# Latent attention block: rotation of q and filler low parts on VectorE, modulation strips in two buffers of their own

## The chip, the core and the metric

One core of a Trainium2 chip runs the kernel: TensorE (PE) for matmuls and transposes, VectorE (DVE), ScalarE (ACT) and GpSimd (POOL) for element work, SyncE (SP) as the queue that issues DMA. The metric is the device time of one execution in microseconds, the median of several.

## The reference

A decoder block on 512 tokens of width 1024, in fp32. A conditioning vector gives six modulation vectors; a merged w_in feeds a latent attention (MLA) and a sparse attention (NSA); a SwiGLU feed-forward (FFN) follows.

```
mod = silu(c) @ ada_w + ada_b                    # 1024 x 6144: shift, scale, gate, twice
h = rms_norm(x) * (1 + sc1) + sh1
z = h @ w_in                                     # c_q 768, c_kv 256, k_pe 32, NSA inputs, two merge gates
q = (rms_norm(c_q) @ w_q_b).reshape(S, 8, 96)    # 64 plain + 32 rotary columns a head
kv = (rms_norm(c_kv) @ w_kv_b).reshape(S, 8, 128)
q, k = rms_norm(q), rms_norm([kv[:64], k_pe])
q[64:96], k[64:96] = apply_rope(...)             # x1*cos - x2*sin, x2*cos + x1*sin
y_mla = causal_attention(q, k, v) @ w_o_mla
merged = sigmoid(g_mla) * y_mla + sigmoid(g_nsa) * y_nsa
x = x + gt1 * (merged @ w_out)
h2 = rms_norm(x) * (1 + sc2) + sh2
x = x + gt2 * ((silu(h2 @ w_gate) * (h2 @ w_up)) @ w_down)
```

## The kernel before

Every fp32 matmul is made of three in a shorter format: an operand is split into a high part (`whi`, `cTh`, `phi`, ..., by ScalarE) and a low part (`wlo`, `cTl`, `plo`, ..., the difference, by VectorE or GpSimd), and high x high, low x high and high x low are added in PSUM. A weight is loaded in pieces of 512 or 384 KB by `wchunk` into a ring of four `raw` buffers (pool `wp`) and split there.

The program runs in stages: modulation and w_in (0 to 162 us of the span), NSA (162 to 304), the latent projections (304 to 362), the eight MLA heads (362 to 452), the output product of MLA and the merge (452 to 484), w_out and the second norm (484 to 536), the FFN (536 to 904). In the projections `latent_cols` transposes the latents (`cTh`, `cTl`), `gk` is the product with w_kv_b and `gq` that with w_q_b, each for two halves c of four heads and four token tiles t. `use_kv` turns a `gk` tile into `msk` (sums of squares), `kn` and `VM`; `use_q` turns a `gq` tile into `jq` (squares, two buffers), `msq` and `qn`. `norm_q` makes the scale `rsq` out of `msq` by a chain of small operations (`rq_i_q`, `rq_h_q`, `rq_m_q`, 128x16 each). In a head, `qh`/`ql` and `kh`/`kl` are the transposed q and k, `ps` the scores, `s`/`mn` the masked scores and their row minimum (a custom operation and a read of its accumulator), `sm` the sums, `av` the values.

Work of other stages is woven in as filler: the merge gates' products (`gp`), the NSA output product (`yn`), and `mods`, the modulation vectors still to come. `fill_lo` chooses the engine for the low parts of a filler's weight, in pieces of 128x512. `mods` goes through 32 strips of 512 KB of ada_w; a strip needs two `macc` operations on VectorE (128x512, accumulator += strip x one element of silu(c) a partition). `E_MODS`, `F_MODS`, `Y_MODS` and `W_MODS` are how many strips the code offers to the projections, heads, merge (twice that) and w_out; `need_mod` runs what is still missing before a vector is used.

The order on each engine is not that of the code: a scheduler that walks through the program with its own estimate of durations sets it, under the dependences and under the pacing of the fillers. Engines and SyncE's queue then work strictly in that order. In the listings L144 before and L143 after are the helper that records every operation of an engine, so its tile names tell operations apart.

Of the kernel before, what the change touches and what calls it, by code (L numbers as in the profile page):

```python
# [35 lines left out]
EF_POOL = 1  # L36
# [5 lines left out]
E_MODS = 4  # L42
F_MODS = 4
GS_BUFS = 1
Y_MODS = 4
W_MODS = 4
# [68 lines left out]
def hybrid_block(ctx, tc, a, out):  # L115
# [152 lines left out]
    def rows(w, r0, parts, c0, n):  # L268
        return w[r0 : r0 + parts * P, c0 : c0 + n].rearrange("(a p) n -> p a n", p=P)

    fill_at = [0, 1]

    def fill_lo():
        fill_at[0] += 1
        return dve if fill_at[0] % fill_at[1] else pool, FILL_CUT
# [618 lines left out]
    strip_src = {}  # L894

    def strip():
        if "pool" in strip_src:
            return strip_src["pool"].tile([P, 1024], F32, name="strip", tag="strip", bufs=1)
        return wp.tile([P, 1024], F32, name="raw", tag="raw")

    mods_done = set()

    def mods():
# [25 lines left out]
        for m, slot in ((2, 4), (3, 2), (4, 3), (5, 5)):  # L929
            done = finish if slot < 4 else finish_row  # L930
            for hf in range(2):
                acc = mcp.tile([P, S], F32, name="macc", tag="macc", bufs=2)
                for r0 in range(0, KD, 2):
                    raw = strip()
                    sp.dma_start(out=raw.rearrange("p (r n) -> p r n", r=2), in_=rows(ada, r0 * P, 2, m * D + hf * S, S))
                    for r in range(2):
                        src = raw[:, r * S : (r + 1) * S]
                        c = csil[:, r0 + r : r0 + r + 1]
                        if r0 + r == 0:
                            dve.tensor_scalar(out=acc, in0=src, scalar1=c, scalar2=None, op0=ALU.mult)  # L940
                        else:
                            dve.scalar_tensor_tensor(out=acc, in0=src, scalar=c, in1=acc, op0=ALU.mult, op1=ALU.add)
                    if r0 == MOD_LAG and late:
                        finish_last(late)
                    yield
                late.append((done, acc, m, slot, hf))
# [115 lines left out]
    fill_at[1] = EF_POOL  # L1062
# [9 lines left out]
    with tc.tile_pool(name="mp", bufs=1, side="right", reuse_waits="tile") as mp:  # L1072
# [36 lines left out]
        def use_q(c):  # L1109
            hs = slice(4 * c, 4 * c + 4)  # L1110

            def f(t, ps):
# [3 lines left out]
                act.activation(out=qn[t][:, hs, :], in_=pv, func=AF.Copy)  # L1116
                dve.tensor_reduce(out=msq[:, c, t, :], in_=jq, axis=AX.X, op=ALU.add)
                rope(pool, qn[t][:, hs, 64:96], c2q[:, t, :], snq[:, t, 16:32], snq[:, t, 0:16], mp, f"q{t}")
# [470 lines left out]
    strip_src["pool"] = fp  # L1589
# [77 lines left out]
```

## Time and profile before

| | us |
|---|---|
| median of 3 runs (lowest to highest) | 907.83 (907.36 to 909.1) |
| profiled execution | 906.09 |
| its span in the trace | 904.0 |
| TensorE busy | 855.2 (95%) |
| VectorE busy | 636.0 (70%) |
| ScalarE busy | 432.4 (48%) |
| GpSimd busy | 176.3 (20%) |

The span is the time from the first to the last record of the trace; the execution's own time has 2.1 us more around it. Busy times are sums over the span. PEclk in the rows below is the TensorE clock that was granted in a stretch, as a share of full speed. "idle before <-releaser" names what ended an engine's wait.

### The profile page before, as it was taken

The page shows a single profiled execution, that of the slowest core. Times are in us where ns is not written, and L with a number is a line of the kernel's source. Part 1 is how long each engine was busy: PE and PEld are TensorE (multiplying, and loading weights), DVE is VectorE, ACT ScalarE, POOL GpSimd, SP SyncE. Part 2 cuts the span into 40 slices and gives each one's busy share as a digit, 9 for nine tenths or more (in the row PEclk, how much of TensorE's full clock was granted, in tenths as well). Part 3 has the DMA queues.
Part 4 walks back from the last instruction along what each step waited for, and adds up shares of the span by engine and source line. Part 5 has one row for each costly group of instructions (what it writes and reads, how often), then busy time and mean ns, then how long its engine had stood idle before and what let it go on. Part 6 is the DMA issues. An engine that isn't in the chain of part 4 may idle for free.

```text
span 904.0 us, 13055 instructions
## 1 busy us (share of the span) xinstructions
PE 855.2 (95%) x4676; PEld 731.4 (81%) x4676; DVE 636.0 (70%) x1288; ACT 432.4 (48%) x863; POOL 176.3 (20%) x222
## 2 busy tenths in 40 slices
PE   5999899899999997999999989999999999999997
PEld 4879899677777786787777878888899889988986
DVE  5857786778976788578779898866754565555644
ACT  5335654787764644466654345341344224431440
POOL 0003335434432037231148014000000000000000
PEclk9999999999999999699999999999999999999999
DMA  9934445321100654135488671553233313342312
GB/s 317 303 98 130 138 140 140 82 71 46 49 12 24 213 150 140 58 106 152 154 293 287 213 229 43 168 163 94 69 106 121 103 53 112 94 119 91 94 47 94
DMA packets 98116, 115.48 MB, mean 128 GB/s; under 512 B 6548, under 2 KB 70660, under 8 KB 98052
## 3 DMA queue, kind: packets, MB, share of 16 engines
q1 hardware_dynamic: 97956, 114.62, 41.3%
q8 instruction: 37, 0.61, 0.3%
q14 instruction: 27, 0.22, 0.1%
q10 hardware_dynamic: 96, 0.03, 0.0%
HBM read 106.24 MB, written 8.39 MB: 127 GB/s over the span
## 4 chain that ended last, share of the span: by engine, by line
PE 73%; DVE 13%; DMA 7%; ACT 2%; issue 2%; SPq 1%; POOL 1%; DVEq 0%; POOLq 0%; ACTq 0%
PE d L144 14%; PE fu L144 13%; PE gp L144 9%; PE fx L144 6%; PE ga L144 5%; PE fy L144 4%; PE pt L144 4%; PE av L144 3%; DMA raw<-in_ada_w_dram 3%; PE fg L144 3%; PE wa L144 2%; DVE macc L144 2%; PE gwo L144 2%; DVE wlo L144 2%; PE ps L144 2%
## 5 line engine op out<-in xcount | busy, mean ns | idle before, releaser
L144 ACT ACTIVATE whi<-raw 128x1024 fp32r<-128x1024 f32 (+4 forms) x162 | 142.1, 892 | 183.0 <-PE d L144 57.8
L144 DVE TENSOR_TENSOR wlo<-raw,whi 128x1024 fp32r<-128x1024 f32 (+3 forms) x122 | 144.0, 1184 | 73.5 <-ACT whi L144 73.1
L144 PE MATMUL fu<-h2l,whi 128*128 128x512 f32 (+1 forms) x192 | 71.3, 372 | 0.0
L144 PE MATMUL fu<-h2h,whi 128*128 128x512 f32 (+1 forms) x192 | 70.7, 372 | 0.0
L144 PE MATMUL fu<-h2h,wlo 128*128 128x512 f32 (+1 forms) x192 | 69.9, 373 | 0.0
L144 PE MATMUL d<-whi,mh 128*128 128x512 f32 x176 | 69.8, 398 | 0.0
L144 PE MATMUL d<-wlo,mh 128*128 128x512 f32 x176 | 69.6, 395 | 0.0
L144 PE MATMUL d<-whi,ml 128*128 128x512 f32 x176 | 67.0, 394 | 0.0
L144 ACT ACTIVATE s<-s,mn 128x384 f32<-128x384 f32 (+2 forms) x96 | 52.5, 548 | 23.0 <-DVE mn L144 22.3
L144 DVE TENSOR_TENSOR plo<-pt,phi 128x512 fp32r<-128x512 f32 (+2 forms) x78 | 46.1, 601 | 21.5 <-ACT phi L144 21.1
L144 POOL TENSOR_TENSOR wlo<-raw,whi 128x512 fp32r<-128x512 f32 x40 | 52.3, 1329 | 44.4 <-ACT whi L144 44.4
L144 PE MATMUL gp<-hTh,whi 128*128 128x512 f32 x128 | 55.4, 433 | 3.7 <-ACT qn L144 3.7
L144 ACT ACTIVATE phi<-pt 128x512 fp32r<-128x512 f32 (+2 forms) x78 | 40.1, 526 | 31.8 <-PE pt L144 31.4
L144 PE MATMUL gp<-hTh,wlo 128*128 128x512 f32 x128 | 52.0, 406 | 0.0
L144 PE MATMUL gp<-hTl,whi 128*128 128x512 f32 x128 | 51.6, 404 | 0.0
L144 DVE SCALAR_TENSOR_TENSOR macc<-raw,csil,macc 128x512 f32<-128x512 f32 x45 | 37.1, 829 | 8.8 <-DMA raw<-in_ada_w_dram 8.3
L144 PEld LDWEIGHTS fu<-h2l,whi 128*128 128x128 f32 x192 | 36.2, 189 | 6.1
L144 PEld LDWEIGHTS fu<-h2h,whi 128*128 128x128 f32 x192 | 35.9, 189 | 6.0
L144 PEld LDWEIGHTS fu<-h2h,wlo 128*128 128x128 f32 x192 | 35.6, 189 | 5.5
L144 PEld LDWEIGHTS d<-whi,mh 128*128 128x128 f32 x176 | 33.0, 188 | 8.2 <-issue 0.2
L144 PEld LDWEIGHTS d<-whi,ml 128*128 128x128 f32 x176 | 33.0, 188 | 8.1
L144 PEld LDWEIGHTS d<-wlo,mh 128*128 128x128 f32 x176 | 33.0, 188 | 7.9 <-issue 0.2
(427 smaller groups left out, 2427.6 us busy)
## 6 DMA issues: line engine op xcount, KB each, us to landing
raw<-in_ada_w_dram SPq DMA_DIRECT2D x26, 512.0 KB, 4.3
raw<-in_ffn_w_gate_dram SPq DMA_DIRECT2D x22, 512.0 KB, 4.7
raw<-in_ffn_w_up_dram SPq DMA_DIRECT2D x22, 512.0 KB, 3.8
raw<-in_ffn_w_down_dram SPq DMA_DIRECT2D x22, 512.0 KB, 4.9
araw<-in_ada_w_dram SPq DMA_DIRECT2D x32, 256.0 KB, 6.3
raw<-in_w_in_dram SPq DMA_DIRECT2D x16, 512.0 KB, 3.9
spill<-gs SPq DMA_DIRECT2D x24, 256.0 KB, 2.0
raw<-in_w_in_dram SPq DMA_DIRECT2D x12, 352.0 KB, 3.2
```

What stands on the lines that cost most here:

```text
L144: out = call(*args, **kw)
```

## The change

`use_q` leaves GpSimd: VectorE multiplies the rotary columns by sine and cosine straight from the PSUM tile `gq` (`rot`, two products of 128x4x16; `qn`, one of 128x4x32) and adds `rot` in SBUF; ScalarE copies only the other 64 columns of each head. On GpSimd these were four operations a tile (`rp_q` twice, two on `qn`), eight tiles. After NSA the low parts of filler weights go to VectorE (16 pieces of 128x512), where GpSimd did them. The strips of `mods` get a pool tag of their own, `strip`, with two buffers, in place of the shared `raw` ring (and of one buffer in a pool of the FFN), and the load of a strip is issued one step before its two `macc`. The numbers of strips offered to the stages change: 4, 4, 2x4, 4 become 0, 16, 2x3, 2.

```diff
--- before.py
+++ after.py
@@ -33,17 +33,16 @@
 YM_AHEAD = 1
 PACE_Y = 8
 FETCH_AHEAD = 4
-EF_POOL = 1
 MOD_LAG = 2
 D_GATES = 88
 E0_GATES = 8
 E_GATES = 0
 F_FILL = 64
-E_MODS = 4
-F_MODS = 4
+E_MODS = 0
+F_MODS = 16
 GS_BUFS = 1
-Y_MODS = 4
-W_MODS = 4
+Y_MODS = 3
+W_MODS = 2
 BIG = 1e30
 QL = 768
 KVL = 256
@@ -268,11 +267,10 @@
     def rows(w, r0, parts, c0, n):
         return w[r0 : r0 + parts * P, c0 : c0 + n].rearrange("(a p) n -> p a n", p=P)
 
-    fill_at = [0, 1]
+    fill_on = [pool]
 
     def fill_lo():
-        fill_at[0] += 1
-        return dve if fill_at[0] % fill_at[1] else pool, FILL_CUT
+        return fill_on[0], FILL_CUT
 
     turn_at = [0]
 
@@ -891,13 +889,6 @@
                         spill(ps, 16 + 2 * i + j)
                     yield
 
-    strip_src = {}
-
-    def strip():
-        if "pool" in strip_src:
-            return strip_src["pool"].tile([P, 1024], F32, name="strip", tag="strip", bufs=1)
-        return wp.tile([P, 1024], F32, name="raw", tag="raw")
-
     mods_done = set()
 
     def mods():
@@ -926,24 +917,33 @@
             pe.matmul(pm, ones, acc, start=True, stop=True)
             dve.tensor_tensor(out=o, in0=pm, in1=o, op=ALU.add)
 
-        for m, slot in ((2, 4), (3, 2), (4, 3), (5, 5)):
-            done = finish if slot < 4 else finish_row
-            for hf in range(2):
+        slots = ((2, 4), (3, 2), (4, 3), (5, 5))
+        jobs = [(m, slot, hf, r0) for m, slot in slots for hf in range(2) for r0 in range(0, KD, 2)]
+
+        def load(job):
+            m, slot, hf, r0 = job
+            raw = mcp.tile([P, 2, S], F32, name="strip", tag="strip", bufs=2)
+            sp.dma_start(out=raw, in_=rows(ada, r0 * P, 2, m * D + hf * S, S))
+            return raw
+
+        ready = load(jobs[0])
+        for i, (m, slot, hf, r0) in enumerate(jobs):
+            raw = ready
+            if i + 1 < len(jobs):
+                ready = load(jobs[i + 1])
+            if r0 == 0:
                 acc = mcp.tile([P, S], F32, name="macc", tag="macc", bufs=2)
-                for r0 in range(0, KD, 2):
-                    raw = strip()
-                    sp.dma_start(out=raw.rearrange("p (r n) -> p r n", r=2), in_=rows(ada, r0 * P, 2, m * D + hf * S, S))
-                    for r in range(2):
-                        src = raw[:, r * S : (r + 1) * S]
-                        c = csil[:, r0 + r : r0 + r + 1]
-                        if r0 + r == 0:
-                            dve.tensor_scalar(out=acc, in0=src, scalar1=c, scalar2=None, op0=ALU.mult)
-                        else:
-                            dve.scalar_tensor_tensor(out=acc, in0=src, scalar=c, in1=acc, op0=ALU.mult, op1=ALU.add)
-                    if r0 == MOD_LAG and late:
-                        finish_last(late)
-                    yield
-                late.append((done, acc, m, slot, hf))
+            for r in range(2):
+                c = csil[:, r0 + r : r0 + r + 1]
+                if r0 + r == 0:
+                    dve.tensor_scalar(out=acc, in0=raw[:, r], scalar1=c, scalar2=None, op0=ALU.mult)
+                else:
+                    dve.scalar_tensor_tensor(out=acc, in0=raw[:, r], scalar=c, in1=acc, op0=ALU.mult, op1=ALU.add)
+            if r0 == MOD_LAG and late:
+                finish_last(late)
+            yield
+            if r0 == KD - 2:
+                late.append((finish if slot < 4 else finish_row, acc, m, slot, hf))
         yield
         yield
         finish_last(late)
@@ -1059,7 +1059,7 @@
     nsa_last = pe.log[-1]
     spill_src.clear()
     pe.pace = 0
-    fill_at[1] = EF_POOL
+    fill_on[0] = dve
     tab_st.close()
 
     mc_st = scope()
@@ -1113,9 +1113,15 @@
                 pv = ps.rearrange("p (h d) -> p h d", h=4)
                 jq = mp.tile([P, 4, MQK], F32, name="jq", tag="jq", bufs=2)
                 act.activation(out=jq, in_=pv, func=AF.Square)
-                act.activation(out=qn[t][:, hs, :], in_=pv, func=AF.Copy)
+                act.activation(out=qn[t][:, hs, 0:64], in_=pv[:, :, 0:64], func=AF.Copy)
+                rot = mp.tile([P, 4, 32], F32, name="rot", tag="rot", bufs=2)
+                heads = lambda v: v.unsqueeze(1).broadcast_to([P, 4, v.shape[-1]])
+                qr = qn[t][:, hs, 64:96]
+                dve.tensor_tensor(out=rot[:, :, 0:16], in0=pv[:, :, 80:96], in1=heads(snq[:, t, 0:16]), op=ALU.mult)
+                dve.tensor_tensor(out=rot[:, :, 16:32], in0=pv[:, :, 64:80], in1=heads(snq[:, t, 16:32]), op=ALU.mult)
+                dve.tensor_tensor(out=qr, in0=pv[:, :, 64:96], in1=heads(c2q[:, t, :]), op=ALU.mult)
+                dve.tensor_tensor(out=qr, in0=qr, in1=rot, op=ALU.add)
                 dve.tensor_reduce(out=msq[:, c, t, :], in_=jq, axis=AX.X, op=ALU.add)
-                rope(pool, qn[t][:, hs, 64:96], c2q[:, t, :], snq[:, t, 16:32], snq[:, t, 0:16], mp, f"q{t}")
             return f
 
         def norm_q(c):
@@ -1586,7 +1592,6 @@
     mg_st.close()
     h2s = ctx.enter_context(tc.tile_pool(name="h2s", bufs=1, reuse_waits="tile"))
     fp = ctx.enter_context(tc.tile_pool(name="fp", bufs=1, side="right", reuse_waits="tile"))
-    strip_src["pool"] = fp
     for k0 in range(0, KD, 4):
         early.append(wchunk(rows(wg, k0 * P, 4, 2 * P, 256), 4, 256))
     sg_first = gu_finish(0, ps_first)
```

What the scheduler makes of it at three places follows. First VectorE at the start of the projections, from the last latent columns (`cTl`) to the first sums of squares (`msk`), before:

```order
L144 SCALAR_TENSOR_TENSOR cTl_3724<-pt,cols_701,cTh_3723 128x512
L144 SCALAR_TENSOR_TENSOR cTl_3760<-pt,cols_701,cTh_3759 128x512
L144 TENSOR_TENSOR wlo<-raw,whi 128x1024
L144 TENSOR_SCALAR macc<-raw,csil 128x512
L144 SCALAR_TENSOR_TENSOR cTl_3745<-pt,cols_701,cTh_3744 128x512
L144 SCALAR_TENSOR_TENSOR macc<-raw,csil,macc 128x512
L144 TENSOR_TENSOR wlo<-raw,whi 128x1024
L144 SCALAR_TENSOR_TENSOR macc<-raw,csil,macc 128x512
L144 TENSOR_REDUCE msk<-jq 128x4
L144 SCALAR_TENSOR_TENSOR VM_3504<-gk_3569,rkv,VM_3504 128x4x64
```

and now, at the same place:

```order
L143 SCALAR_TENSOR_TENSOR macc<-strip,csil,macc 128x512
L143 SCALAR_TENSOR_TENSOR cTl_3719<-pt,cols_701,cTh_3718 128x512
L143 SCALAR_TENSOR_TENSOR cTl_3755<-pt,cols_701,cTh_3754 128x512
L143 SCALAR_TENSOR_TENSOR macc<-strip,csil,macc 128x512
L143 TENSOR_TENSOR wlo<-raw,whi 128x1024
L143 SCALAR_TENSOR_TENSOR cTl_3740<-pt,cols_701,cTh_3739 128x512
L143 TENSOR_TENSOR wlo<-raw,whi 128x1024
L143 TENSOR_TENSOR wlo<-raw,whi 128x768
L143 SCALAR_TENSOR_TENSOR macc<-strip,csil,macc 128x512
L143 TENSOR_SCALAR macc<-strip,csil 128x512
L143 SCALAR_TENSOR_TENSOR macc<-strip,csil,macc 128x512 x2
L143 TENSOR_REDUCE msk<-jq 128x4
```

With four further up, two of them ahead of the first `cTl`, six `macc` stand now ahead of the first `wlo`, and ten ahead of the first `msk`; before it was none and three.

Second SyncE's queue at the end of NSA, where w_kv_b for the projections is loaded. Before:

```order
L924 DMA gt_4638<-in_ada_b_dram 128x512 x2
L257 DMA raw<-in_mla_w_kv_b_dram 128x2x512
L935 DMA raw<-in_ada_w_dram 128x2x512
L864 DMA spill_1847<-gs 128x512
L257 DMA raw<-in_mla_w_kv_b_dram 128x2x512
L935 DMA raw<-in_ada_w_dram 128x2x512
L257 DMA raw<-in_mla_w_q_b_dram 128x2x384 x3
```

and now:

```order
L926 DMA strip<-in_ada_w_dram 128x2x512 x2
L915 DMA gt_4517<-in_ada_b_dram 128x512 x2
L926 DMA strip<-in_ada_w_dram 128x2x512
L256 DMA raw<-in_mla_w_kv_b_dram 128x2x512 x2
L862 DMA spill_1847<-gs 128x512
L256 DMA raw<-in_mla_w_q_b_dram 128x2x384
L926 DMA strip<-in_ada_w_dram 128x2x512
```

Three strips stand now ahead of w_kv_b; the third needs a buffer that the first one's two `macc` give back.

Third VectorE up to the first score operation (`ISA s`) of the first head. Before, its last rows:

```order
L144 SCALAR_TENSOR_TENSOR ql<-pt,cols_701,qh 96x512
L144 TENSOR_TENSOR rq_m_q_4281<-rq_i_q_4279,rq_h_q_4280 128x16
L144 TENSOR_TENSOR rq_m_q_4281<-rq_m_q_4281,rq_i_q_4279 128x16
L144 SCALAR_TENSOR_TENSOR kl<-pt,cols_701,kh 96x512
L144 SCALAR_TENSOR_TENSOR rsq<-rq_m_q_4281,rq_i_q_4279 128x16
L144 SCALAR_TENSOR_TENSOR macc<-raw,csil,macc 128x512 x2
L144 ISA s_4136,mn<-ps,mask,rsq 128x128
```

and now, the rows from the scale `rsq` of the first four heads on, as far as the second four's `msq`:

```order
L143 SCALAR_TENSOR_TENSOR rsq<-rq_m_q_3926,rq_i_q_3924 128x16
L143 TENSOR_TENSOR wlo<-raw,whi 128x512 x4
L143 TENSOR_REDUCE msq<-jq 128x4
L143 TENSOR_TENSOR rot<-gq_3940,snq 128x4x16 x2
L143 TENSOR_TENSOR qn_3498<-gq_3940,c2q 128x4x32
L143 TENSOR_REDUCE msq<-jq 128x4
L143 TENSOR_TENSOR rot<-gq_3941,snq 128x4x16 x2
L143 TENSOR_TENSOR qn_3499<-gq_3941,c2q 128x4x32
L143 TENSOR_TENSOR wlo<-raw,whi 128x512
L143 TENSOR_TENSOR qn_3498<-qn_3498,rot 128x4x32
L143 TENSOR_TENSOR wlo<-raw,whi 128x512
L143 SCALAR_TENSOR_TENSOR msq<-msq,vq 128x16
```

The two `macc` in front of the score are gone from that place; six `wlo` of filler weights and the rotation of the last two `gq` tiles stand now between `rsq` and the scores. Counted over the whole of VectorE's order, `macc` operations up to the first MLA score operation are 16 (14 before), up to the first `gm` 44 (30), the last `gm` 48 (34), the first `tm` 56 (40), the first `xs` 64 (52); there are 64 in all.

## Rows read from the trace of the kernel before

**Rows 1.** The page's head: the span, busy time of each engine (share of the span, instructions), and the chain that ended last by engine.

```profile
span 904.0 us, 13055 instructions
...
PE 855.2 (95%) x4676; PEld 731.4 (81%) x4676; DVE 636.0 (70%) x1288; ACT 432.4 (48%) x863; POOL 176.3 (20%) x222
...
PE 73%; DVE 13%; DMA 7%; ACT 2%; issue 2%; SPq 1%; POOL 1%; DVEq 0%; POOLq 0%; ACTq 0%
```

**Rows 2.** Busy time of each engine in stretches of the span: start and end, length, then busy time and number of instructions of each engine, the granted clock, the busy share of DMA, GB/s.

```profile
304.00:362.00 58.00, 48.78 (x248) 42.61 (x246) 52.24 (x124) 30.41 (x66) 24.52 (x40) 0.97 0.54 164
362.00:452.00 90.00, 85.19 (x440) 70.14 (x441) 63.10 (x157) 54.37 (x134) 18.94 (x18) 0.92 0.38 118
...
480.00:536.00 56.00, 50.54 (x227) 40.61 (x225) 52.51 (x76) 24.20 (x42) 15.46 (x10) 0.97 0.75 240
...
610.00:904.00 294.00, 289.37 (x1578) 250.09 (x1576) 169.59 (x231) 94.33 (x123) 0.00 (x0) 1.00 0.30 92
```

**Rows 3.** VectorE's timeline, first half of the projections: start, duration, operation, number of them, and in brackets the idle time before and what ended it.

```profile
300.36 2.07 DVE L144 SCALAR_TENSOR_TENSOR cTl<-pt,cols,cTh 128x512 fp32r<-128x512 f32 x3 [1.15 <-ACT cTh L144]
304.13 2.73 DVE L144 SCALAR_TENSOR_TENSOR cTl<-pt,cols,cTh 128x512 fp32r<-128x512 f32 x4 [1.71 <-ACT cTh L144]
...
309.01 0.74 DVE L144 SCALAR_TENSOR_TENSOR macc<-raw,csil,macc 128x512 f32<-128x512 f32 x1
309.70 1.23 DVE L144 TENSOR_TENSOR wlo<-raw,whi 128x1024 fp32r<-128x1024 f32 x1
...
312.01 0.48 DVE L144 SCALAR_TENSOR_TENSOR VM<-gk,rkv,VM 128x256 fp32r<-128x256 f32 x1
...
317.87 0.75 DVE L144 SCALAR_TENSOR_TENSOR macc<-raw,csil,macc 128x512 f32<-128x512 f32 x1 [0.49 <-DMA raw<-in_ada_w_dram]
...
326.88 0.75 DVE L144 SCALAR_TENSOR_TENSOR macc<-raw,csil,macc 128x512 f32<-128x512 f32 x1 [2.23 <-DMA raw<-in_ada_w_dram]
...
328.58 0.90 DVE L144 TENSOR_TENSOR kn<-kpr,rsk 128x128 f32<-128x128 f32 x4
...
329.73 1.43 DVE L144 TENSOR_TENSOR kn<-kn,rsk 128x256 f32<-128x256 f32 x4
331.08 1.15 DVE L144 TENSOR_TENSOR kn<-kpr,rsk 128x128 f32<-128x128 f32 x4
...
335.28 2.06 DVE L144 TENSOR_TENSOR kn<-kn,rsk 128x256 f32<-128x256 f32 x4
```

**Rows 4.** The same, second half, up to the first score operation (CUSTOM_DVE_ANT_0).

```profile
341.56 0.17 DVE L144 SCALAR_TENSOR_TENSOR rq_i_q<-rq_m_q,rq_i_q 128x16 f32<-128x16 f32 x1
341.77 1.31 DVE L144 TENSOR_TENSOR rq_m_q<-rq_i_q,rq_h_q 128x16 f32<-128x16 f32 x1
343.11 1.22 DVE L144 TENSOR_TENSOR rq_m_q<-rq_m_q,rq_i_q 128x16 f32<-128x16 f32 x1
344.36 1.21 DVE L144 SCALAR_TENSOR_TENSOR rq_i_q<-rq_m_q,rq_i_q 128x16 f32<-128x16 f32 x1
345.61 1.20 DVE L144 TENSOR_TENSOR rq_m_q<-rq_i_q,rq_h_q 128x16 f32<-128x16 f32 x1
...
356.35 0.38 DVE L144 TENSOR_TENSOR rq_m_q<-rq_m_q,rq_i_q 128x16 f32<-128x16 f32 x1
...
359.50 2.41 DVE L144 SCALAR_TENSOR_TENSOR macc<-raw,csil,macc 128x512 f32<-128x512 f32 x2
361.83 0.34 DVE L144 CUSTOM_DVE_ANT_0 s<-ps,mask,rsq 128x128 f32<-128x128 f32 x1
```

**Rows 5.** GpSimd's timeline in the same stretch.

```profile
341.75 5.03 POOL L144 TENSOR_TENSOR wlo<-raw,whi 128x512 fp32r<-128x512 f32 x4 [1.36 <-ACT whi L144]
...
359.91 3.14 POOL L144 TENSOR_TENSOR wlo<-raw,whi 128x512 fp32r<-128x512 f32 x2 [1.95 <-ACT whi L144]
```

**Rows 6.** TensorE's timeline: the matmuls behind its two longest waits.

```profile
350.43 0.50 PE L144 MATMUL gp<-hTh,whi 128*128 128x512 f32 x1 [3.69 <-ACT qn L144]
...
362.23 0.69 PE L144 MATMUL ps<-kh,qh 96*128 96x384 f32 x1 [2.85 <-DVE mn L144]
```

**Rows 7.** Busy times by stretch, as in rows 2, in shorter stretches.

```profile
350.00:362.00 12.00, 8.96 (x38) 7.02 (x38) 9.68 (x21) 6.30 (x12) 9.08 (x16) 0.86 0.56 177
362.00:376.00 14.00, 12.76 (x39) 10.33 (x40) 8.43 (x27) 6.56 (x19) 2.52 (x3) 0.51 0.29 94
376.00:400.00 24.00, 23.63 (x137) 20.10 (x136) 13.15 (x33) 14.33 (x35) 7.05 (x6) 1.00 0.21 67
520.00:536.00 16.00, 12.77 (x69) 10.46 (x67) 15.69 (x34) 9.37 (x17) 1.76 (x2) 1.00 0.84 254
536.00:563.00 27.00, 24.83 (x204) 24.39 (x204) 22.93 (x46) 13.06 (x23) 10.35 (x9) 1.00 0.19 59
```

**Rows 8.** VectorE's groups of instructions from 304 to 452 by shape: number | busy, mean ns | idle before.

```profile
L144 DVE TENSOR_TENSOR wlo<-raw,whi 128x1024 fp32r<-128x1024 f32 x5 | 6.1, 1223 | 0.0
...
L144 DVE TENSOR_TENSOR plo<-pt,phi 128x512 fp32r<-128x512 f32 x8 | 5.5, 686 | 1.5 <-ACT phi L144 1.4
```

**Rows 9.** What VectorE waited for in the heads, 362 to 452: us in total, times, longest.

```profile
DVE macc L144 <- DMA raw<-in_ada_w_dram: 5.6, 4, 2.1
```

**Rows 10.** The chain that ended last, from 508 to 530: start, duration, what.

```profile
511.19 4.81 DMA raw<-in_ada_w_dram
...
518.53 1.42 DVE macc L144 x2
```

## The prediction

> **What bounds the kernel now.** I read the page first: TensorE is busy 855.2 of 904.0 us and holds 73% of the chain, VectorE 13%, DMA 7% [rows 1]. An average of 95% hides where the loss is, so the busy times by stretch come second [rows 2]. From 610 on TensorE has 289.37 of 294 us: nothing that this change does can shorten that. In the latent projections (304 to 362) it is TensorE that waits, 48.78 of 58, while VectorE has 52.24; in the attention heads (362 to 452) TensorE has 85.19 of 90 at a mean granted clock of 0.92; between 480 and 536 VectorE (52.51 of 56) is again the fuller one. So the price of the change is read on VectorE in the projections, and on TensorE's waits and clock behind them.
>
> VectorE's line through the projections [rows 3, 4] runs from the first `cTl` at 300.36 to the first score operation at 361.83: 61.5 us. In it stand idle times of 1.71 (for ScalarE), 0.49 and 2.23 us (a `macc` waiting for its strip's DMA). And it has operations that are far longer than their kind: `rq_m_q` on 128x16 takes 0.17 us and follows at 0.21 us (341.56 to 341.77), but the next four take 1.31, 1.22, 1.21 and 1.20 us, exactly while GpSimd runs four `wlo` in 5.03 us [rows 5]. The two `macc` before the first score take 2.41 us where one alone follows at 0.69 (309.01 to 309.70); GpSimd has two `wlo` there. I read that as the two engines being in each other's way.
>
> TensorE shows what this costs [rows 6]: it waits 3.69 us at 350.43 for ScalarE's `qn`, which was late because VectorE had not freed `jq`, and 2.85 us at 362.23 for the first score operation. After the second wait the granted clock is 0.51 until 376, and 1.00 again after that [rows 7]: its half level, 1.2 of 2.4 GHz.
>
> **The change, part by part.**
>
> *Rotation on VectorE.* Eight tiles, each with two 64-element products, one 128-element product (all three from PSUM) and one 128-element sum. No row shows them. Nearest: `kn` 128x128 follows at 0.21 (0.90 for four, less the overlap), 128x16 at 0.08 to 0.21, `VM` 128x256 from PSUM 0.48. Below: 2x0.08+0.21+0.21=0.58 a tile; above: 2x0.2+0.4+0.2+0.2=1.2. I take 0.74, near `kn`, the likest shape: 8x0.74=+5.9 (ends 4.6 and 9.6).
>
> The Trainium skill ("Perfetto Trace Analysis", Optimizing Scalar/DVE Operations) gives about 60 ns of access overhead for VectorE on SBUF and about 125 ns on PSUM, which speaks against this part. For 24 PSUM operations that would be an estimated +1.6 us, and the sum below would be -7.4 instead of -9. The trace has `VM` at 0.48 for 256 elements against about 0.34 for `kn` (1.43 for four, overlap off), which agrees in sign, over different operations.
>
> *Low parts on VectorE.* The order has six 512-column `wlo` ahead of the first score that GpSimd had before. At half of a 1024 (1.22/2) to a `plo` of 128x512 (0.69) [rows 8] I take 0.6: +3.6. One `kl` (0.7) and two 0.2 us operations pass behind the score: -1.1. `macc` from the first `cTl` to the score is 14 before and 14 after, so it adds nothing; but four of the fourteen (and two ahead of the first `cTl`) now stand before the first low part of `w_kv_b`, which before had none: they fill the 1.71 us that VectorE idles there and push the rest by about 1.1 us (4x0.69-1.71).
>
> *GpSimd leaves.* Its 24.52 us in this stretch [rows 2] were rotations and `wlo`, so the interference goes: the four `rq` operations 5.07-0.84=4.2, the last `macc` pair 2.33-1.33=1.0, four `kn` 1.98-1.35=0.6 (335.28 against 329.73), and twelve smaller pieces from the `kn` at 331.08 (four in 1.15 us, 0.90 at 328.58) to the `rq_m_q` at 356.35 (0.38), which I sum to 2.9 by the same subtraction [rows 3, 4]: -8.7 (ends -5.8 without the small ones, -8.7).
>
> *Strips a step ahead.* The waits of 0.49 and 2.23 us should go, and the 1.71 fills: -4.4. New waits, for ScalarE's `qh` or for the banks that VectorE's rotation now holds longer: I take +1.5 (ends 0 and 4).
>
> Sum to the first score: +5.9+3.6-1.1-8.7-4.4+1.5=-3.2, call it -3. All favourable ends together give -6, all unfavourable +6. In front of both `w_kv_b` loads SyncE now has a third strip, whose buffer waits for `macc` on VectorE; I put the load some 5 us later, TensorE's first `gk` about 1 us later. TensorE has 9.2 us of idle in the stretch to hide it, VectorE's line has it inside the 1.1 above.
>
> *The clock behind it.* From 362 to 376 TensorE is 12.76 us busy at half clock. At full clock this is about half, but VectorE's 8.43 us are in the way [rows 7]: the stretch would take about 9, so -5. The condition is that the 2.85 us wait before the third score matmul shrinks: TensorE's fillers ahead of it are the same, the score operation comes 3 us earlier, and no `macc` stands before it. I think it falls to about 1.5 us. Ends: 0 (the wait stays as long) and -6.4.
>
> *Heads.* From the first score to the first `gm`, VectorE gets 28 `macc` for 16 and 8 more `wlo`: 12x0.67+8x0.6=12.8 us, on 63.10 of 90. This lies beside TensorE's work, with 14 us left; without that cover it costs up to 12.8. The four waits for strips (5.6 us [rows 9]) partly go. I take +1 (ends 0 and +5).
>
> *Merge and w_out.* Four `macc` stay between the first and the last `gm`; from there to the first `tm` 8 for 6, from there to `xs` 8 for 12. The chain there holds a 4.81 us DMA wait and a pair of `macc` 1.42 us [rows 10]. Gain on VectorE: 2x0.67 plus the wait; but TensorE idles only 3.2 and 2.2 us between 520 and 563 [rows 7], which is the ceiling. I take -2 (ends 0 and -5.4). The last 12 `macc` leave the first FFN stretch (536 to 610), where they waited beside a full TensorE: 0.
>
> Sum: -3-5+1-2=**-9**: span 895.0, profiled execution 897.1 against 906.09; on the median 907.83, **898.8**. A measurement of this kernel can tell about 0.2% (1.8 us) from no change.
>
> **Rivals.**
>
> *The low clock stays.* If the wait before the third score stays near its present length, -5 becomes 0: 903.8. For it: VectorE comes only 3 us earlier, and 2.85 and 3.69 us of waiting were both followed by a drop. Against: no `macc` ahead of the score. The mechanism is the same, the gain half.
>
> *The projections don't get shorter (the change doesn't do what it says).* If the rotation costs 1.2 a tile and the new waits 4 us, the first sum is -3+3.7+2.5=+3; the clock stays too: 907.8+3+1-2=909.8. The point is 1.1 us a tile. For it: VectorE is already the fullest engine here.
>
> *VectorE ends up as the bound in the heads: slower.* Fourteen strips pass there instead of 8, with two buffers, so a strip can be asked for only when the one before the last is consumed. If each waits 2.07 us, as before's longest, that is 29 us against the 14 left: +15, less the -3 of the projections and -2 of w_out, with the clock unimproved: about 917; at 1.5 us each 21-14=7 and about 910. It decides from 1 us a strip. Against: before, 8 strips waited 5.6 us, 0.7 each, without loading ahead.
>
> **How the numbers follow.** Forecast case 0.45 (its own range 891 to 903, from the bounds with the clock recovered at least in part); low clock stays 0.25 (900 to 907); projections not shorter 0.14 (905 to 911); heads bound 0.16 (908 to 918). The range of 889 to 909.5 leaves out most of the last case and the far tail. Faster by over 0.2% (below 906.0): 0.45+0.20+0.03+0.01=0.69. Within: 0.04+0.05+0.01=0.10. Slower: the rest, 0.21.
>
> **What would show it.** Right: four `rq_m_q` of 0.2 us in a row, first score operation near 358 to 359, TensorE's wait before the third score about 1.5 us, granted clock 1.00 from 362 to 376, no DMA wait above 2 us before `xs`. Wrong: rotation operations over 0.3 us, `macc` waiting for its strip in most heads, TensorE waiting for `mn` or `plo` there, or a stretch at half clock somewhere else between 304 and 480, above all behind a new TensorE wait in the projections.

## The result: 0.54% slower

| | before | changed |
|---|---|---|
| median of 20 runs each (lowest to highest) | 907.37 us (904.24 to 909.21) | 911.92 us (907.81 to 916.09) |
| ratio, 95% interval | | 1.0054 (1.0040 to 1.0068) |
| profiled execution / its span | 906.09 / 904.0 | 910.04 / 908.2 |

Forecast was 898.8, between 889 and 909.5. The measured time lies outside, and on the other side of no change.

The head of the page of the changed kernel answers to [rows 1]:

```profile
span 908.2 us, 13045 instructions
...
PE 856.2 (94%) x4676; PEld 733.2 (81%) x4676; DVE 640.1 (70%) x1336; ACT 431.6 (48%) x863; POOL 138.9 (15%) x174
...
PE 77%; DVE 8%; DMA 7%; ACT 3%; issue 2%; SPq 2%; POOL 1%; DVEq 0%; ACTq 0%
```

TensorE has the same work (856.2 against 855.2 us), VectorE 4 us more, GpSimd 37 us less. VectorE's share of the chain fell from 13% to 8%, and yet the span is 4.2 us longer. Busy times by stretch, as in [rows 2]:

```profile
304.00:362.00 58.00, 51.00 (x251) 45.04 (x251) 51.34 (x165) 29.44 (x67) 0.00 (x0) 0.94 0.58 185
362.00:452.00 90.00, 83.23 (x451) 68.35 (x451) 73.77 (x176) 55.50 (x135) 10.82 (x11) 0.98 0.44 138
```

In the projections TensorE is fuller than before (51.00 of 58 us for 48.78), in the heads VectorE has 73.77 us for 63.10. What was lost shows in places in the program, not in fixed windows. I use four lengths, from the first and last start of a product by the trace's summaries and from the first score operation: **projections**, first `gk` to last `gq`; **heads**, first score operation to first `gym`; **merge**, first `gym` (the output product of MLA) to last `gwo` (the product of the merged result with w_out); **second norm and first FFN products**, last `gwo` to first `d` (the product with w_down).

| | projections | first score at | heads | merge | norm, FFN |
|---|---|---|---|---|---|
| before | 38.7 | 361.8 | 90.8 | 53.2 | 102.0 |
| changed | 43.6 | 359.3 | 91.5 | 61.8 | 99.9 |

The account of the profiled execution: first score -2.5, heads +0.7, merge +8.6, norm and first FFN products -2.1, the rest -0.5: together +4.2.

VectorE in the projections of the changed kernel, answering to [rows 3, 4] (start, duration, operation, idle before):

```profile
314.92 0.48 DVE L143 TENSOR_SCALAR macc<-strip,csil 128x512 f32<-128x512 f32 x1 [3.17 <-DMA strip<-in_ada_w_dram]
...
316.65 0.41 DVE L143 TENSOR_REDUCE msk<-jq 128x4 f32<-128x256 f32 x1
```

```profile
343.00 0.35 DVE L143 TENSOR_TENSOR rot<-gq,snq 128x64 f32<-128x64 f32 x2
343.27 0.28 DVE L143 TENSOR_TENSOR qn<-gq,c2q 128x128 f32<-128x128 f32 x1
...
343.55 0.49 DVE L143 TENSOR_TENSOR qn<-qn,rot 128x128 f32<-128x128 f32 x2
...
347.55 0.18 DVE L143 SCALAR_TENSOR_TENSOR rq_i_q<-rq_m_q,rq_i_q 128x16 f32<-128x16 f32 x1
347.76 0.17 DVE L143 TENSOR_TENSOR rq_m_q<-rq_i_q,rq_h_q 128x16 f32<-128x16 f32 x1
...
349.38 2.50 DVE L143 TENSOR_TENSOR wlo<-raw,whi 128x512 fp32r<-128x512 f32 x4 [1.02 <-ACT whi L143]
...
359.34 0.35 DVE L143 CUSTOM_DVE_ANT_0 s<-ps,mask,rsq 128x128 f32<-128x128 f32 x1
```

The chain `rq` runs at 0.21 us a step now (347.55 to 347.76), where before it took 1.2 us beside GpSimd. The rotation is `rot` twice in 0.35 us and 0.20 us for the product from PSUM (343.27 to 343.47) and for each sum. The first score comes at 359.34. But ahead of the first `msk` a `macc` waits 3.17 us for its strip, and TensorE pays, answering to [rows 6]:

```profile
307.22 1.21 PE L143 MATMUL gk<-whi,cTh 128*128 128x512 f32 x4 [2.56 <-ACT whi L143]
...
317.50 0.50 PE L143 MATMUL gk<-whi,cTh 128*128 128x512 f32 x1 [2.54 <-DVE VM L143]
```

Of the waits at 350.43 and 362.23 before, 0.95 and 1.26 us are left. The clock, answering to [rows 7]:

```profile
307.00:315.00 8.00, 7.70 (x24) 5.56 (x24) 4.83 (x7) 4.47 (x10) 0.00 (x0) 0.79 0.99 337
318.00:323.00 5.00, 5.00 (x17) 3.91 (x16) 4.67 (x11) 3.71 (x11) 0.00 (x0) 0.66 0.78 271
...
362.00:376.00 14.00, 11.24 (x59) 8.67 (x59) 9.01 (x26) 7.02 (x20) 1.41 (x2) 1.00 0.17 56
...
470.00:478.00 8.00, 5.96 (x19) 4.63 (x19) 5.82 (x7) 4.71 (x8) 7.84 (x6) 0.79 0.98 337
488.00:497.00 9.00, 7.41 (x25) 6.02 (x26) 7.60 (x11) 2.30 (x4) 6.11 (x5) 0.62 0.48 152
```

It is full from 362 to 376, as forecast. It is half, 1.2 of 2.4 GHz, for a part of 307 to 315, of 318 to 323 and of 470 to 478, and for most of 488 to 497. In the merge before there was one such stretch:

```profile
484.00:489.00 5.00, 5.00 (x17) 3.90 (x16) 4.96 (x5) 3.71 (x7) 4.50 (x3) 0.66 0.83 281
```

In the merge of the changed kernel the chain goes through these pieces (start, duration, what; `pm` is the small product that closes an accumulator of `macc`):

```profile
456.89 8.83 DMA yn<-spill
...
469.26 2.30 DVE wlo L143
...
479.59 1.78 DVE macc L143
...
486.62 1.78 DVE macc L143
...
488.53 1.06 PE pm L143 x8
```

and TensorE waits there (us in total, times, longest) 8.3 us:

```profile
PE gym L143 <- DVE gm L143: 4.0, 2, 2.0
PE gwo L143 <- DVE gm L143: 3.2, 2, 2.1
PE pm L143 <- DVE macc L143: 1.1, 1, 1.1
```

where before it was 2.7:

```profile
PE gwo L144 <- DVE wlo L144: 2.2, 1, 2.2
PE gym L144 <- DVE gm L144: 0.5, 1, 0.5
```

These are 5.6 us of the 8.6. The clock can be the rest: one minus the granted clock, times the length, is 1.7 and 3.4 us in the two stretches of the changed kernel and 1.7 us in the one before, so by this estimate 3.4 us more; the two together come to 9.0 us, a little over what there is to explain.

### The profile page after: what moved, and what is told of

The parts are those of the page before. It is cut to its first block, busy times and chain, and to the rows that moved or that the text cites. A ratio compares the mean times of both kernels' runs of the same rounds, so it can differ in the third digit from the quotient of the medians.

```text
span 908.2 us, 13045 instructions
## 1 busy us (share of the span) xinstructions
PE 856.2 (94%) x4676; PEld 733.2 (81%) x4676; DVE 640.1 (70%) x1336; ACT 431.6 (48%) x863; POOL 138.9 (15%) x174
## 4 chain that ended last, share of the span: by engine, by line
PE 77%; DVE 8%; DMA 7%; ACT 3%; issue 2%; SPq 2%; POOL 1%; DVEq 0%; ACTq 0%
PE d L143 14%; PE fu L143 13%; PE gp L143 8%; PE fx L143 6%; PE ga L143 5%; PE fy L143 4%; PE pt L143 4%; PE av L143 3%; DMA araw<-in_ada_w_dram 3%; PE gq L143 3%; PE fg L143 2%; PE gwo L143 2%; PE yn L143 2%; PE wo L143 2%; DVE s L143 2%
## 5 line engine op out<-in xcount | busy, mean ns | idle before, releaser
L143 DVE TENSOR_TENSOR wlo<-raw,whi 128x1024 fp32r<-128x1024 f32 (+4 forms) x138 | 153.1, 1117 | 93.3 <-ACT whi L143 92.9
L143 DVE SCALAR_TENSOR_TENSOR macc<-strip,csil,macc 128x512 f32<-128x512 f32 x56 | 45.7, 818 | 2.5 <-DMA strip<-in_ada_w_dram 2.1
L143 POOL TENSOR_SCALAR s<-s,sm 128x512 f32<-128x512 f32 (+3 forms) x40 | 25.0, 639 | 142.6 <-DVE sm L143 123.6
```

Source lines behind the costliest of these rows:

```text
L143: out = call(*args, **kw)
```

## The experiments

Twelve kernels, each timed against the kernel before on the same chip. Theories on the way: **strips** (the loss comes from where the strips and their `macc` went), **load** (VectorE can't carry GpSimd's work), and, within the first, **start** (early strips), **queue** (SyncE's order at the end of the heads), **merge** (strips inside the merge), **buffers** or **numbers**.

| kernel | median us | ratio to before (95%) | projections | heads | merge | norm, FFN |
|---|---|---|---|---|---|---|
| rotation alone | 902.77 | 0.9950 (0.9927 to 0.9972) | 40.3 | 88.5 | 53.0 | 103.7 |
| low parts alone | 901.70 | 0.9929 (0.9899 to 0.9958) | 38.4 | 89.2 | 53.1 | 104.7 |
| strips alone | 920.85 | 1.0144 (1.0114 to 1.0175) | 40.8 | 96.1 | 60.4 | 103.1 |
| rotation and low parts | 905.83 | 0.9977 (0.9957 to 0.9998) | 40.4 | 88.7 | 53.1 | 102.0 |
| changed, x later | 915.24 | 1.0083 (1.0053 to 1.0112) | 42.4 | 92.9 | 60.2 | 102.7 |
| changed, start | 917.51 | 1.0110 (1.0082 to 1.0137) | 44.3 | 94.9 | 62.1 | 99.9 |
| changed, old numbers | 921.42 | 1.0138 (1.0112 to 1.0163) | 40.8 | 87.4 | 59.8 | 114.3 |
| changed, x later and start | 916.12 | 1.0084 (1.0061 to 1.0108) | 44.0 | 94.8 | 59.5 | 103.8 |
| changed, hold | 910.07 | 1.0027 (1.0007 to 1.0047) | 41.8 | 94.2 | 54.0 | 103.3 |
| changed, ring | 911.09 | 1.0035 (1.0013 to 1.0058) | 37.9 | 95.3 | 59.7 | 101.2 |
| rotation, low parts, four jq | 904.03 | 0.9946 (0.9920 to 0.9971) | 38.7 | 90.4 | 53.1 | 102.2 |
| low parts, four jq | 900.71 | 0.9916 (0.9893 to 0.9939) | 37.2 | 89.9 | 53.0 | 103.4 |

The lengths are from one profiled execution each and hold whatever the clock did there; what stands out are the merge (53.0 to 54.0 or 59.5 to 62.1, nothing between) and the heads (87.4 to 90.8 with the old numbers of strips, 91.5 to 96.1 with more strips offered to the heads, the changed kernel at the lower end).

### The parts one by one

Each part is put into the kernel before. Rotation alone:

```diff
-                act.activation(out=qn[t][:, hs, :], in_=pv, func=AF.Copy)
+                act.activation(out=qn[t][:, hs, 0:64], in_=pv[:, :, 0:64], func=AF.Copy)
+                dve.tensor_tensor(out=rot[:, :, 0:16], in0=pv[:, :, 80:96], in1=heads(snq[:, t, 0:16]), op=ALU.mult)
...
-                rope(pool, qn[t][:, hs, 64:96], c2q[:, t, :], snq[:, t, 16:32], snq[:, t, 0:16], mp, f"q{t}")
```

> The kernel before with the rotation of q alone on VectorE; low parts of fillers stay on GpSimd, strips stay in the raw ring with the old numbers. Strips theory (the loss of the changed kernel comes from the strips: six macc ahead of the first low part of w_kv_b in the projections, and SyncE's queue and the DMA at the end of the heads): this part alone is not slower, -1 to -3 us against before, because GpSimd's rotations no longer lie beside VectorE's work. Load theory (the loss comes from putting GpSimd's work on VectorE, which is the fullest engine in the projections): +2 to +4 us.

Low parts alone:

```diff
-    fill_at[1] = EF_POOL
+    fill_on[0] = dve
```

> The kernel before with the fillers' low parts alone on VectorE after NSA. Strips theory: -2 to -4 us against before, since the four rq operations of 1.2 us beside GpSimd's low parts go back to 0.2 us. Load theory: 0 to +3 us.

Strips alone, the buffers and the load ahead with the new numbers:

```diff
-E_MODS = 4
-F_MODS = 4
+E_MODS = 0
+F_MODS = 16
...
-                    raw = strip()
+            raw = mcp.tile([P, 2, S], F32, name="strip", tag="strip", bufs=2)
```

> The kernel before with the strips alone changed: own two buffers, loaded a step ahead, 0, 16, 2x3, 2 strips to the stages. Strips theory: slower than before by 4 us or more, with TensorE's two waits of 2.5 us at the first gk products and waits for gm in the merge as in the changed kernel. Load theory: faster, -2 to -4 us, as the DMA waits of macc go.

Rotation and low parts together, without the strips:

> Rotation and low parts on VectorE, strips as before: GpSimd is idle from the projections on until the heads. Strips theory: -4 to -6 us against before, last gq product not later than 346. Load theory: +4 us or more, last gq product after 349.

Rotation -0.50%, low parts -0.71%, strips +1.44%: of the two, the strips theory holds and the load theory falls. The sizes were missed: both single parts gained more than was expected, the two together less (-1.9 us for -4 to -6, and the last `gq` at 346.3). The strips alone cost 13 us, more than in company; in their heads the clock was half for some 24 us, where before it was 14. With low parts alone the `rq` operations are short again although the rotation is still on GpSimd (that kernel's VectorE timeline: start, duration):

```profile
344.32 0.18 DVE L143 TENSOR_TENSOR rq_m_q<-rq_i_q,rq_h_q 128x16 f32<-128x16 f32 x1
344.53 0.17 DVE L143 TENSOR_TENSOR rq_m_q<-rq_m_q,rq_i_q 128x16 f32<-128x16 f32 x1
```

The rotation is not free for TensorE. Alone it makes the first `gq` product of the second half wait, and the first head's transposes (the waits of the kernel with the rotation alone: us in total, times, longest):

```profile
PE gq L144 <- ACT jq L144: 3.0, 1, 3.0
PE pt L144 <- DVE msq L144: 2.5, 1, 2.5
```

The projections take 40.3 us against 38.4 with low parts alone. Both together gained only 0.23% where 1.2% would be the sum. The profiled execution of that kernel had a span of 899.0 and is faster than its median of 905.83; no single place in it shows the missing 9 us, and why the two gains don't add stays open.

### The start and the queue

x later: the loads of x follow the last merge fetch on SyncE's queue.

```diff
-        sp.dma_start(out=x2[t], in_=a["x"][0, t * P : (t + 1) * P, :])
+        follow_dma(sp.dma_start(out=x2[t], in_=a["x"][0, t * P : (t + 1) * P, :]).ins, fetched[-1])
```

> The changed kernel, but the four loads of x for the residual (512 KB each) are issued behind the last merge fetch (gm, gs, yn) on SyncE's queue. Queue theory (strips that wait for macc hold up SyncE's queue at the end of the heads, the x loads go out late, and the merge's first fetch shares the DMA with them and lands late): the merge, from the first gym to the last gwo product, goes from 61.8 us back to 53 to 55, as in the kernels with the old strips (53.0 to 53.2); about -6 us against the changed kernel, 903 to 907. VectorE theory (two w_out low parts between the first gm operations and macc among them, beside GpSimd's yn, make the merge long): merge stays at 60 to 62, no change of the time.

What suggested it is SyncE's queue in the changed kernel (start, duration of the issue, what):

```profile
445.61 3.66 SPq L926 DMA_DIRECT2D strip<-in_ada_w_dram  x2
449.35 0.42 SPq L1330 DMA_DIRECT2D x<-in_x_dram  x1
451.99 0.37 SPq L926 DMA_DIRECT2D strip<-in_ada_w_dram  x1
452.45 1.21 SPq L1330 DMA_DIRECT2D x<-in_x_dram  x2
...
454.23 0.60 SPq L1330 DMA_DIRECT2D x<-in_x_dram  x1
...
455.46 0.76 SPq L1307 DMA_DIRECT2D gm<-spill  x1
```

Two strips hold the queue for 3.66 us until a `macc` gives a buffer back, the x loads follow behind them at 449.35 to 454.23 (before all four went out from 448.10 on), and the first fetch of the merge, at 455.46, shares the DMA with 2 MB of x: a `yn` fetch takes 8.83 us in the chain above. With x later the `gym` products are back at the length of before: 26.0 us from first to last start where the changed kernel took 30.6 (before 26.1). The rows are a tile's summary (number, duration in ns least/median/most, first and last start). In the changed kernel:

```profile
L143 PE MATMUL gym<-omh,whi x32: 389/397/720, 450.8 to 481.4; 128*128 128x512 f32 x32
```

and with x later:

```profile
L143 PE MATMUL gym<-omh,whi x32: 389/392/501, 459.4 to 485.4; 128*128 128x512 f32 x32
```

But the `gwo` products behind them stretch, from 27.7 us in the changed kernel:

```profile
L143 PE MATMUL gwo<-whi,mTl x32: 394/399/628, 484.9 to 512.6; 128*128 128x512 f32 x32
```

to 33.0 with x later,

```profile
L143 PE MATMUL gwo<-whi,mTl x32: 392/392/628, 486.6 to 519.6; 128*128 128x512 f32 x32
```

so that the merge stays at 60.2. TensorE's timeline of that kernel shows two of the waits:

```profile
491.89 0.49 PE L143 MATMUL gwo<-whi,mTl 128*128 128x512 f32 x1 [2.41 <-DVE mTl L143]
494.44 1.84 PE L143 MATMUL pm<-ones,macc 128*128 128x1 f32 x8 [2.06 <-DVE macc L143]
```

They are for VectorE's `mTl`, and then `pm`, the small product that closes an accumulator, stands between two `gwo` products in TensorE's queue and waits for the last `macc`. The loads of x do lie in the way of the first fetches, and moving them alone is worth nothing.

Start: no strip ahead of w_kv_b.

```diff
+            follow_dma(ins, kv_last[0])
             return raw
```

> The changed kernel, but no strip is loaded ahead of w_kv_b's second piece on SyncE's queue, so that only 2 macc, not 10, stand ahead of the first msk. Start theory (the early strips cost the projections their 5 us, by TensorE's waits of 2.56 and 2.54 us and the half clock behind each): last gq product at 346 to 347 and -3 to -5 us against the changed kernel. Rival (the rotation on VectorE sets the projections): last gq product stays at 350 or later, no change.

The start theory falls as it was put. The projections take 44.3 us. The first `gk` waits go (the wait for `VM` is absent, the one for `whi` is 1.24), but the strip's wait only moves. VectorE in this kernel:

```profile
332.70 0.75 DVE L143 SCALAR_TENSOR_TENSOR macc<-strip,csil,macc 128x512 f32<-128x512 f32 x1 [3.19 <-DMA strip<-in_ada_w_dram]
...
337.50 0.55 DVE L143 TENSOR_REDUCE msq<-jq 128x4 f32<-128x384 f32 x1
```

and TensorE in the same kernel:

```profile
338.65 0.66 PE L143 MATMUL gq<-whi,cTh 128*128 128x384 f32 x1 [4.93 <-ACT jq L143]
```

A `macc` waits 3.19 us for its strip in front of the `msq`, ScalarE waits for `msq` to give `jq` back, and TensorE for ScalarE. Not all of the 4.93 us is the strip's: the same product waits 3.03 us in the kernel with the rotation alone and 2.76 us with rotation and low parts. The rest, about 2 us, came when the early strips were moved, and the rival fares no better: the ring kernel below has the rotation on VectorE too, and its last `gq` product starts at 344.6.

Old numbers: the buffers and the load ahead stay, the numbers are those of before.

```diff
-E_MODS = 0
-F_MODS = 16
+E_MODS = 4
+F_MODS = 4
-Y_MODS = 3
-W_MODS = 2
+Y_MODS = 4
+W_MODS = 4
```

> The changed kernel with the old numbers of strips, 4, 4, 2x4, 4, in place of 0, 16, 2x3, 2; the two own buffers and the load a step ahead stay. In its order no strip stands among the x loads; 28 macc up to the first gm instead of 44. Queue theory: merge 53 to 55 us, -6 us against the changed kernel. If the buffers and the load ahead are the cause: merge stays at 60 or more.

The numbers are not the cause of the merge (59.8). They are of the heads: 12 `macc` from the first score to the first `gm` instead of 28, and 87.4 us instead of 91.5, with half clock for about 3.4 us in both. But the `macc` that are left then stand ahead of the second norm, and TensorE waits there, in this kernel's timeline:

```profile
547.45 1.94 PE L143 MATMUL pt<-ident,xs 128*128 128x128 f32 x8 [13.21 <-DVE rq_m_x L143]
```

Both holds, x later and no strip ahead of w_kv_b, in one kernel:

> Both edits together, x later and no strip ahead of w_kv_b. Start and queue theory together: -9 to -11 us against the changed kernel, 900 to 903. If one of them falls, its share is missing.

It has neither share: merge 59.5, projections 44.0, and 916.12 us.

### Strips out of the merge, and the ring

Hold: no strip is offered to the merge, 20 to the heads; strips 20 to 31 follow the last merge fetch and are loaded at their own step, with one buffer for those in the FFN.

```diff
-F_MODS = 16
-Y_MODS = 3
-W_MODS = 2
+F_MODS = 20
+Y_MODS = 0
+W_MODS = 4
+HOLD = 20
...
+            if jobs.index(job) >= HOLD:
+                follow_dma(ins, fetched[-1])
```

> The changed kernel, but strips 20 to 31 go out on SyncE only behind the last merge fetch, and the last six of them are loaded in the FFN as in the kernel before: no macc stands between the first and the last gm, and no pm between two gwo products. Merge theory (strips, their macc and the pm that waits for them make the merge long): first gym to last gwo 53 to 55 us instead of 61.8, projections as in the changed kernel (42 to 44 us); 901 to 906 if the second norm doesn't pay it back. Rival (the two w_out low parts between the first two gm, beside GpSimd's yn): merge 58 or more.

This settles that the strips made the merge long: 54.0 us, with the low parts of w_out still between the first two `gm`. `gym` takes 25.1 us and `gwo` 23.2 in this kernel:

```profile
L144 PE MATMUL gym<-omh,whi x32: 389/389/501, 453.1 to 478.2; 128*128 128x512 f32 x32
```

and

```profile
L144 PE MATMUL gwo<-whi,mTl x32: 392/393/628, 483.9 to 507.1; 128*128 128x512 f32 x32
```

Of the 7.8 us, the norm behind it takes 3.4 back (103.3 against 99.9), about half of it by half clock from 538 to 542 (0.61 and 0.54 granted), and the heads were 2.7 longer in this execution, with 24 `macc` in them for 23: 910.07, still slower than before, and not the 901 to 906 that a merge without strips could have given.

Ring: the strips in the raw ring of four again, new numbers and the load ahead kept.

```diff
-            raw = mcp.tile([P, 2, S], F32, name="strip", tag="strip", bufs=2)
+            raw = wp.tile([P, 1024], F32, name="raw", tag="raw").rearrange("p (r n) -> p r n", r=2)
```

> The changed kernel with the strips in the shared raw ring of four again; the numbers of strips and the load a step ahead stay as changed. In its order no macc stands ahead of the first msk (10 in the changed kernel). Buffer theory (the two own buffers let the strips be put early): projections 40 to 41 us as with rotation and low parts alone; the merge keeps its pm between two gwo products, so 58 to 62; 905 to 910 in all. Rival (the numbers are the cause): projections 43 or more.

Projections 37.9: without buffers of their own no strip comes early, and the 5 us are gone. The merge stays long, now by the closing product (the waits of the ring kernel in the merge: us in total, times, longest):

```profile
PE pm L143 <- DVE macc L143: 4.0, 1, 4.0
PE gwo L143 <- DVE gm L143: 2.4, 1, 2.4
```

With heads of 95.3 us the time is 911.09, just above what was expected. So the early strips come with the buffers. The long merge comes with old and new numbers, with two buffers and with the ring. What its seven kernels share is a `pm` between two `gwo` products; the seven kernels with a merge of 53.0 to 54.0 have none there. In the kernel before, for one, it stands between the `gym` products and waits for nothing, and the next is at 506.00, behind the last `gwo`:

```profile
473.05 0.95 PE L144 MATMUL pm<-ones,macc 128*128 128x1 f32 x8
```

That the `pm` alone does it is not shown: its own wait is 1.1 to 4.0 us, or none that the trace shows (strips alone), and no run moves it without moving strips and `macc`.

### Four jq buffers

```diff
-                jq = mp.tile([P, 4, MQK], F32, name="jq", tag="jq", bufs=2)
+                jq = mp.tile([P, 4, MQK], F32, name="jq", tag="jq", bufs=4)
```

> Rotation and low parts on VectorE with the old strips, and four jq buffers for two. If the wait of 2.8 to 3.0 us of the first gq product of the second half comes from jq (ScalarE waits for VectorE's msq), it goes and the projections take 38 us instead of 40.4; 902 to 904. If the bank of gq that VectorE's rotation reads holds it, nothing changes: 40 us, 905 to 907.

> Low parts alone on VectorE with the old strips, and four jq buffers for two. The jq theory: the 2.5 us wait of the first filler for qn shrinks, 899 to 901. Otherwise 901 to 903, as low parts alone.

Four buffers for `jq`, once with rotation and low parts, once with the low parts alone. With the rotation, the wait in the second half of `gq` is 1.36 us (2.8 with two buffers) and the projections take 38.7 us (40.4); TensorE's timeline of that kernel:

```profile
335.51 0.42 PE L143 MATMUL gq<-whi,cTh 128*128 128x384 f32 x1 [1.36 <-ACT qn L143]
```

So `jq` was about half of it. What is left ends, within 0.01 us, both with a copy of ScalarE (335.37) and with VectorE's first rotation (335.36), so that the bank may hold the rest; no run separates the two. The time of 904.03 us is not clear of the 905.83 with two buffers. With the low parts alone the wait of 2.50 us of the first filler is gone, as the theory had it. That kernel is the fastest here, 900.71 us, 0.84% faster than before; against low parts alone (0.71%) the intervals overlap.

## Why the prediction was wrong

**Projections, first score -3: right, by luck.** -2.5 measured. The interference left as forecast (`rq` back at 0.21 us), the rotation follows at 0.27 (two `rot`), 0.20 and 0.20, 0.67 a tile where I took 0.74, the six low parts 2.50 us for four, 0.62 each, where I took 0.6. The strips' waits did not go. -4.4 and +1.5 stood in the sum for VectorE's waits, -2.9 together; from the first `cTl` to the first score its idle time fell only from 6.5 to 6.0 us, with a new wait of 3.17 us. What made up for it: its work there shrank by 1.4 us, where my other terms give -0.3, and the first `cTl` came 0.6 us earlier (299.75 for 300.36), for which I had no term. A load "a step ahead" with two buffers can't go out before the `macc` of the strip before the last, and the 3.17 us show that this was too late. One reading was wrong besides: `VM` at 0.48 against `kn` at 0.34 compares a duration with a distance from start to start, and two kinds of operation.

**TensorE's side of the projections: the step failed.** I wrote that its 9.2 us of idle would hide a first `gk` about 1 us later. The first `gk` came 0.4 us later, but the last `gq` 5.3 us later, with two waits of 2.56 and 2.54 us and a stretch of half clock behind each, the last of my signs of being wrong. It cost little in the end: the first score, which hangs on VectorE, came earlier all the same.

**The clock behind it, -5: mechanism right, price probably too high.** The wait fell to 1.26 us and the clock was full from 362 to 376. What that is worth shows best in the kernel with the old numbers, which has as little half clock in its heads as the changed one: 87.4 us against 90.8, -3.4, with four `macc` fewer and the low parts added. Without the strips (rotation, low parts, both) it was about -2, with half clock left for 7 to 10 us.

**Heads, +1: mis-sized.** Changed against old numbers, 28 `macc` for 12, is 91.5 against 87.4: +4.1, near my upper end of 5, and 91.5 is the lowest of the kernels with that many strips there. Together with the clock the term came out at -3.4+4.1=+0.7 instead of -4. My rival for the heads needed 1 us of wait a strip; the price came without it. What VectorE waited for in the heads of the changed kernel, answering to [rows 9]:

```profile
DVE macc L143 <- DMA strip<-in_ada_w_dram: 1.5, 2, 1.1
```

So the load ahead works here, 1.5 us of waiting for 5.6. VectorE is 73.77 us busy of 90, and TensorE's waits for its `plo` rose from 0.2 to 1.2 us; for the other microseconds I have no row, and their cause stays open.

**Merge, 0: the step that turned the sign.** +8.6. I counted `macc` between the first and last `gm`, found four before and four now, and priced the stage at nothing. That term, put at nothing because a count had not changed, is the step that failed. What I did not read in the order: the strips' loads now stood among the x loads on SyncE's queue just ahead of the merge's fetches, and a `pm` stood between two `gwo` products, where before one stood between the `gym` products and the next behind the last `gwo`. TensorE's waits there grew by 5.6 us, and the half clock took about 3.4 us more by the estimate above. The hold kernel, which takes strips, `macc` and `pm` out of there, has 54.0; of the three, the loads alone are ruled out by the kernel with x later, as far as they lie among those of x, and `macc` and `pm` are not separated. Of the 13.2 us between the forecast (-9) and the profiled span (+4.2), the merge has 8.6 and the heads with their clock 4.7.

**Norm and w_out, -2: right** (-2.1). The chain there no longer goes through the load of a strip, and VectorE's longest wait for one from 500 to 560 is 0.9 us, for 1.7 before.

**The rivals.** None named the merge. The slower rival, VectorE as the bound in the heads, had the right sign, and its stage did cost 4.1 us against the old numbers, but not by the waits of 1 us a strip that it needed.

## What to carry to other kernels

A transfer that is issued ahead into few buffers can still be paid for where its consumer stands in an in-order queue: ask for every row between the consumer and the next thing someone waits for, not how many consumers a stage has. When a scheduler is free to hoist, an extra pool of buffers can move work to where there is no room for it; compare each stage's order, queue by queue, also the stages that the counts say are unchanged. And time the parts of a combined change apart: here two of three parts were gains of 0.5% and 0.7% (together 0.23%, and why they don't add stays open), and the third cost twice as much as the larger gain.

## What the runs showed of the hardware

The price of VectorE and GpSimd working at once is large for operations on two SBUF inputs: the `macc` at 479.59 took 1.78 us where 0.74 is usual, in the time of this GpSimd operation (start, duration):

```profile
478.67 2.16 POOL L143 TENSOR_TENSOR yn<-yn,gm 128x512 f32<-128x512 f32 x1
```

The Trainium skill ("SBUF — State Buffer", Who interferes with whom) says that a VectorE instruction with two SBUF inputs contends with a GpSimd instruction that reads SBUF, and that the port pair the two share is an exclusive lock. The trace agrees: the `macc` runs beside that GpSimd operation for 1.24 us and is 1.04 us longer, while the next `macc`, at 482.99, with GpSimd idle, took 0.74.

A wait alone does not decide about TensorE's clock. In the changed kernel waits of 2.56 and 2.54 us were followed by half clock, as 2.85 us were before; but the wait of 3.0 us in the kernel with the rotation alone, and one of 2.8 us with rotation and low parts, were followed by a granted clock of 1.00 in the ten microseconds behind. My forecast of the clock rested on the length of one wait.

A product from PSUM was no dearer on VectorE than the sum in SBUF of the same size: 0.20 us each from start to start (343.27 to 343.47, and two sums in 343.55 to 343.95). What did differ is the operation: on 128x512 `scalar_tensor_tensor` follows at 0.66 us from PSUM (`cTl` at 308.35 before) and from SBUF (`macc` at 310.84 before), `tensor_tensor` at 0.60 (`gm` at 490.77 before, from PSUM; the four `wlo` at 349.38, from SBUF, 0.61).
